# Hybrid attention and recurrence layer: half of the embedding's product moves from attention to the first up products, and six other places are reordered

## The chip, the cores and the metric

The kernel runs on one core of a Trainium2 chip. The metric is the device time of one execution in microseconds (us), the median of some runs. A core has TensorE (PE; its weight loads are PEld), VectorE (DVE), ScalarE (ACT), GpSimd (POOL) and SyncE (SP, which issues the DMAs here). They run side by side and wait for each other by semaphores. Each works through its own instructions in order.

## The reference

One layer on 1024 tokens of width 1024, all in float32:

```
h = rms(x);  c_q, c_kv, k_rope, lru_x, lru_gate = split(h @ w_in)
q, k, v from c_q and c_kv (8 heads, 64 + 32 rotary), RMS norm of q and k per head
attn = softmax(q k^T / sqrt(96), chunk mask) v
lru  = scan(a, b) * gelu(lru_gate)          a, b from two sigmoid gates of conv4(lru_x)
x = x + concat(rms(attn), rms(lru)) @ w_out
x = x + (gelu(g) * v) @ w_down              g, v = conv3(rms(x) @ w_up), 2 x 2816 wide
x = x + sigmoid(rms(x) @ w_gate + b) * (p @ w_ple)       p: 1024 x 256
```

The last product, p @ w_ple, depends on nothing else in the layer. It is called the embedding here.

## The kernel before

Everything is held transposed: 128 features on the partitions, tokens along a row, in two halves of 512 tokens. A float32 operand is split into a high part (`hi`, a ScalarE copy) and a rest (`lo`, a VectorE subtraction), and each product is three matmuls per block of 128 x 128 x 512: hi hi, hi lo, lo hi (`split`, `three`, `chain`, lines 108 to 145). `chain` issues nearly all matmuls, so they carry line 108, and the tile's name tells them apart.

The stages follow each other in `build`. `project` loads x, scales and splits it, adds up its squares (line 255), and multiplies with w_in; `lru` within it runs the recurrent block in four chunks of 128 channels; `qkv` makes queries, keys and values for eight tiles of tokens. `attention` runs eight heads. Per head it transposes q and k (`turn`), makes scores and softmax for eight tiles of queries (`probs`), transposes the probabilities (`turn_probs`) and weighs the values (`weigh`). These are jobs with a time in units, 12 of them for a head (`TURN_AT`, `PROBS_AT`, `BLOCK_AT`, `WEIGH_AT`), and a sort by time gives the order in which they are written. The embedding is among the jobs: `embed(c, h)`, for each of eight blocks c of 128 features and each half h of the tokens, at -1.0 and 3.25 of a head's 12 units. It has 6 matmuls of 512 columns, a copy by ScalarE (line 1197) and a store of 256 KB (line 1198); the results wait in memory until the last stage. `mix` multiplies with w_out: for each half and each of eight blocks, a product over the recurrent part (`lru`), one over the attention part (`at`), each scaled by VectorE and added to x1.

`ffn` makes the up product by seven products instead of eight for each pair of output blocks (Strassen with sums): `order` lists them as (pair u, product 1 to 7). `weights` and `finish_weights` (`W`, `W2`) prepare the w_up operand A, `operand` and `T(n, k)` the x operand B, `sums` adds the products to the outputs U, `run` does a product with its sums. The first 15 products are written out by hand around the operands. `down` runs 22 steps in each half, over eight accumulators that fill all of PSUM, with operands loaded two steps ahead (`load_down`); after a half, `gained` scales and splits x for the last stage, for all eight blocks. `ple` is the gate product, 16 of 24 matmuls. A scale of the RMS norm goes `measure` (TensorE, VectorE, GpSimd: 1/sqrt) and `scale` (VectorE makes a diagonal tile dg, TensorE spreads it, ScalarE copies).

The order written is not the order run in every case. A scheduler in the framework takes the instructions with their priority in the order written, works with estimated durations, gives each engine whatever is ready in that estimate, and assigns buffers. Tiles of one tag share a ring of `bufs` buffers: tag "sq" has 4 (`NTMP`), "wraw" 3, "whi" and "wlo" 2 each, "B" 12. PSUM has eight banks; `banks` names them by stage, and "big" tiles take two.

Of the kernel before, what the change touches and what calls it, by code (L numbers as in the profile page):

```python
# [11 lines left out]
F32 = mybir.dt.float32  # L12
# [34 lines left out]
EMBED_AT = (-1.0, 3.25)  # L47
# [27 lines left out]
class Block:  # L75
# [137 lines left out]
    def project(self):  # L213
# [22 lines left out]
        for k in range(NK):  # L236
# [13 lines left out]
            if k == 0:  # L250
                nc.scalar.activation(ssum, raw, AF.Square)
            else:
                sq = rp.tile([P, S], F32, tag="xsq", name="xsq", bufs=2)
                nc.scalar.activation(sq, raw, AF.Square)
                (nc.gpsimd if k % 2 and k < NK - 1 else nc.vector).tensor_tensor(out=ssum, in0=ssum, in1=sq, op=ALU.add)
# [119 lines left out]
    def lru(self, x, ws, done, then, scale):  # L375
# [43 lines left out]
        for c in range(NL):  # L419
# [131 lines left out]
    def qkv(self, t, c, uq, ukv):  # L551
# [31 lines left out]
        if t == NT - 1:  # L583

            nc.scalar.activation(tmp, tmp, AF.Exp, scale=0.0)
# [20 lines left out]
    def attention(self):  # L606
# [11 lines left out]
        self.pp = [self.wload(self.i["pT"][k]) for k in range(2)]  # L618
        self.e = []
# [6 lines left out]
        mask = self.w.tile([P, S], F32, tag="wraw", name="mask", bufs=3)  # L626
        nc.sync.dma_start(out=mask[QK:QK + NT], in_=self.i["mask"][0])
        for g in range(2):
            nc.scalar.copy(self.qb[g][0][QK:QK + NT], mask[QK:QK + NT, g * HALF:(g + 1) * HALF])
        mask = self.w.tile([P, S], F32, tag="wraw", name="mask", bufs=3)  # L630
        nc.sync.dma_start(out=mask[QK:QK + NT], in_=self.i["mask"][1])
        for g in range(2):
            nc.scalar.copy(self.kb[g][0][QK:QK + NT], mask[QK:QK + NT])
# [4 lines left out]
        jobs = []  # L638
# [19 lines left out]
        self.mix_attn(3, 0)  # L658
# [87 lines left out]
    def mix(self):  # L746
# [13 lines left out]
        for h in range(2):  # L760
# [8 lines left out]
            for c in range(NK + 2):  # L769
                if c < NK:  # L770
# [13 lines left out]
                if c >= 2:  # L784
                    o, x = at[c - 2], self.x1[c - 2][h]
                    V.tensor_tensor(out=o, in0=o, in1=self.r1[:, hs], op=ALU.mult)
                    V.tensor_tensor(out=x, in0=o, in1=x, op=ALU.add)
                    nc.sync.dma_start(out=self.xs[c - 2][:, hs], in_=x)
                    self.square(("x1", h), c - 2, x)
                if h == 1:  # L790
                    if c == 2:
                        self.measure("x1", 0, D)
                        for z, u in ((0, 0), (1, 0), (0, 1)):
                            self.fetch(u, z)
                    if c == 3:

                        self.scale("x1", 0)
                    if 4 <= c < 8:
                        for k in (c - 4, c):
                            self.normed(k, 0)  # L800
                            self.operand(("B21" if k >= NL else "B11", k % NL), self.x1[k][0], self.m[0])
                            self.finish_operand()
# [216 lines left out]
    def ffn(self):  # L1019
# [48 lines left out]
        run(2)  # L1068
        run(3)
        T(1, 0)  # L1070
        T(1, 1)
        W2(7)
        T(1, 2)
        T(1, 3)
# [3 lines left out]
        W2(8)  # L1078
        run(5)
# [72 lines left out]
    def down(self):  # L1152
# [29 lines left out]
    def embed(self, c, h):  # L1182
# [132 lines left out]
```

## Time and profile before

| | |
|---|---|
| median of 3 runs | 1242.09 us (1239.92 to 1243.95) |
| profiled execution: own time, span | 1244.59 us, 1242.8 us |
| VectorE, ScalarE, GpSimd busy | 72%, 52%, 13% of the span |
| mean granted clock of TensorE | 0.984 of full speed |
| DMA | 128.78 MB, 30% of 16 engines' span |

All times of rows are from the start of the span. TensorE's busy time counts matmuls whose ends are modelled and which overlap, so a matmul of 0.39 us may be issued every 0.23. The stages lie about so: front and input products to 164 us, `qkv` to 198, attention to 370, mix to 467, up products to 899, down to 1145, gate to the end.

### The profile page before, as it was taken

Reading aid. Unit: us, or ns where it says so; the run is one execution under the profiler, and the core shown is the slowest. Engines: PE = TensorE matmul, PEld = TensorE weight load, DVE = VectorE, ACT = ScalarE, POOL = GpSimd, SP = SyncE. Lnnn points to the kernel's source line nnn. Section 1 sums busy time; section 2 is a strip of 40 time slices with the busy share of each in tenths; the row PEclk is TensorE's granted clock in tenths of the full one; section 3 lists DMA queues with packets and bytes.
Section 4 is the critical chain, followed back from the end, with each engine's and each line's share of the span. In section 5 each row is a group of like instructions: output and inputs, shape, how many; then the busy total and the mean of one; then the engine's idle time right before and its main releaser. Section 6 shows DMA issues by size and latency. Waiting matters only on the chain.

```text
span 1242.8 us, 15388 instructions
## 1 busy us (share of the span) xinstructions
PE 1201.3 (97%) x5600; PEld 1001.7 (81%) x5600; DVE 896.6 (72%) x1406; ACT 643.6 (52%) x1030; POOL 165.8 (13%) x180
## 2 busy tenths in 40 slices
PE   7999998999999998899999999999999998999998
PEld 5787986888878887788888888888888886888787
DVE  7879798777778699998878878778653346444633
ACT  7388677888874134654544545545432244333211
POOL 3012264444430000000000000000000021001200
PEclk9999998999999998899999999999999998999999
DMA  6213200111168220322222222122485336641221
GB/s 226 68 55 111 103 7 9 48 36 55 43 196 291 86 73 22 107 97 85 85 85 85 69 102 85 68 88 86 132 286 186 106 103 219 202 153 51 69 101 69
DMA packets 49932, 128.78 MB, mean 104 GB/s; under 512 B 5808, under 2 KB 8752, under 8 KB 49856
## 3 DMA queue, kind: packets, MB, share of 16 engines
q1 hardware_dynamic: 49856, 127.80, 30.2%
q8 instruction: 44, 0.72, 0.2%
q14 instruction: 32, 0.26, 0.1%
HBM read 97.36 MB, written 28.31 MB: 101 GB/s over the span
## 4 chain that ended last, share of the span: by engine, by line
PE 66%; DVE 6%; issue 1%; DMA 0%; ACT 0%; POOL 0%; POOLq 0%; DVEq 0%
PE b L108 31%; PE dn L108 16%; PE gt L108 6%; PE lru L108 4%; PE at L108 3%; PE st L108 2%; DVE m L118 1%; DVE B L911 1%; PE big L108 1%; DVE x L1038 1%; DVE x L1177 1%; DVE x L896 0%; PE p L734 0%; PE st L144 0%; DMA om<-oc 0%
## 5 line engine op out<-in xcount | busy, mean ns | idle before, releaser
L108 PE MATMUL b<-B,A 128*128 128x512 f32 x1848 | 424.9, 392 | 3.7 <-DVE U L992 3.4
L108 PEld LDWEIGHTS b<-B,A 128*128 128x128 f32 x1848 | 349.7, 190 | 78.0 <-issue 3.8
L108 PE MATMUL dn<-m,whi 128*128 128x512 f32 x616 | 191.9, 392 | 4.9 <-DVE m L113 4.9
L113 DVE TENSOR_TENSOR wlo<-wraw,whi 128x1024 fp32r<-128x1024 f32 (+2 forms) x59 | 68.1, 1157 | 123.8 <-ACT whi L112 123.8
L108 PEld LDWEIGHTS dn<-m,whi 128*128 128x128 f32 x616 | 116.8, 190 | 29.9 <-DVE m L113 5.4
L112 ACT CAST whi<-wraw 128x1024 fp32r<-128x1024 f32 (+2 forms) x59 | 58.4, 994 | 147.0 <-PE st L108 136.7
L108 PE MATMUL dn<-m,wlo 128*128 128x512 f32 x308 | 120.9, 392 | 0.0
L1004 DVE SCALAR_TENSOR_TENSOR u<-U,par,u 128x1023 f32<-128x1023 f32 x88 | 112.4, 1278 | 2.1 <-ACT u L1009 2.0
L846 POOL TENSOR_TENSOR ssum<-ssum,sq 128x512 f32<-128x512 f32 x14 | 21.4, 1532 | 658.7 <-ACT sq L842 657.9
L944 ACT CAST A<-s 128x512 fp32r<-128x512 f32 x88 | 54.7, 622 | 78.0 <-PE b L108 70.8
L108 PE MATMUL gt<-m,wh 128*128 128x512 f32 (+1 forms) x272 | 80.0, 377 | 0.0
L108 PE MATMUL big<-kT,qT 96*128 96x384 f32 (+11 forms) x288 | 68.7, 365 | 3.5 <-ACT kT L117 3.3
L952 DVE TENSOR_TENSOR A<-s,A 128x512 fp32r<-128x512 f32 x88 | 60.6, 689 | 14.7 <-ACT A L944 14.6
L108 PEld LDWEIGHTS dn<-m,wlo 128*128 128x128 f32 x308 | 58.5, 190 | 12.1
L972 ACT COPY keep<-b 128x512 f32<-128x512 f32 x66 | 38.4, 583 | 52.4 <-PE b L108 52.4
L702 DVE TENSOR_SCALAR_CACHE_REDUCE pr<-big,nrq 128x512 f32<-128x512 f32 (+3 forms) x64 | 51.9, 814 | 11.7 <-PE p L715 4.3
L706 POOL TENSOR_SCALAR pr<-pr,st 128x512 f32<-128x512 f32 (+3 forms) x64 | 48.2, 757 | 78.5 <-DVE st L705 59.9
L944 ACT CAST A<-wraw 128x512 fp32r<-128x512 f32 x54 | 33.4, 622 | 47.8 <-PE b L108 40.5
L108 PEld LDWEIGHTS big<-kT,qT 96*128 96x128 f32 (+1 forms) x288 | 50.3, 198 | 9.1 <-ACT kT L117 3.8
L108 PEld LDWEIGHTS gt<-m,wh 128*128 128x128 f32 x272 | 50.0, 188 | 9.3
L1009 ACT ACTIVATE u<-U,par 128x1024 f32<-128x1024 f32 x44 | 54.7, 1246 | 1.5 <-DVE U L994 0.4
L704 ACT ACTIVATE pr<-pr,st 128x512 f32<-128x512 f32 (+3 forms) x64 | 49.7, 777 | 8.0 <-DVE pr L702 6.8
(327 smaller groups left out, 2289.8 us busy)
## 6 DMA issues: line engine op xcount, KB each, us to landing
wraw<-w_down SPq DMA_DIRECT2D x44, 512.0 KB, 3.4
wraw<-w_up SPq DMA_DIRECT2D x33, 512.0 KB, 3.3
g<-u SPq DMA_DIRECT2D x22, 512.0 KB, 2.6
graw<-g SPq DMA_DIRECT2D x44, 256.0 KB, 4.1
raw<-w_up SPq DMA_DIRECT2D x11, 512.0 KB, 3.4
e<-eo SPq DMA_DIRECT2D x16, 256.0 KB, 2.4
m<-y SPq DMA_DIRECT2D x8, 512.0 KB, 7.2
x<-xT SPq DMA_DIRECT2D x16, 256.0 KB, 7.0
```

Of the source, the lines that this page charges most:

```text
L108: self.nc.tensor.matmul(out, lhsT=w, rhs=x, start=start and n == 0, stop=stop and n == len(terms) - 1, **kw)
L112: self.nc.scalar.copy(hi, src)
L113: (self.nc.gpsimd if pool else self.nc.vector).tensor_tensor(out=lo, in0=src, in1=hi.bitcast(F32), op=ALU.subtract)
L702: V.tensor_scalar(out=pv, in0=sc, scalar1=self.nrq[:, qt, h:h + 1], scalar2=None, op0=ALU.mult, op1=ALU.min, accum_out=st[:, 0:1])
L704: nc.scalar.activation(pv, pv, AF.Exp, bias=st[:, 0:1], scale=-1.0, accum_out=st[:, 1:2])
L706: nc.gpsimd.tensor_scalar(out=pr[:, :kend], in0=pr[:, :kend], scalar1=st[:, 2:3], scalar2=1.0, op0=ALU.mult, op1=ALU.mult)
L846: (nc.gpsimd if pool else nc.vector).tensor_tensor(out=self.ssum[key], in0=self.ssum[key], in1=sq, op=ALU.add)
L944: self.nc.scalar.copy(t[:, :HALF], src)
L952: self.nc.vector.tensor_tensor(out=lo, in0=src, in1=hi.bitcast(F32), op=ALU.subtract)
L972: self.nc.scalar.copy(t, self.bank[u, b])
L1004: tap = lambda z, d: V.scalar_tensor_tensor(out=self.u[u, z][:, d:], in0=self.U[u, z][:, :S - d], scalar=self.col(f"cw{2 - d}", z * NF + u ...
L1009: nc.scalar.activation(t, self.U[u, n], AF.Identity, bias=self.col("cb", n * NF + u), scale=self.col("cw2", n * NF + u))
```

## The change

Half 1 of the embedding leaves attention: `embed(c, 1)` now runs in `ffn`, two blocks at a time, between `run(1)` and `run(5)`, from its own load and split of w_ple. p is loaded by halves (`embedded`). The six other places:

1. The front's sum of squares is added by VectorE alone; GpSimd did three of the seven adds.
2. In the last chunk of `lru`, the second gate's two halves go into one "big" accumulator with one sigmoid.
3. The load of Exp's table (an activation that does nothing else) and two of the four casts of the mask come as jobs behind the first two turns.
4. In `mix`, the `at` product runs one block behind the `lru` product, `mix_attn(3, 0)` comes within the mix, and the scale of x1's first half and its operands come earlier.
5. In `down`, the first half's `gained` is spread over steps 1 to 8 of the second half.
6. In `ple`, the scales come one product later.

```
-EMBED_AT = (-1.0, 3.25)
+EMBED_AT = -1.0
 ...
-                (nc.gpsimd if k % 2 and k < NK - 1 else nc.vector).tensor_tensor(out=ssum, in0=ssum, in1=sq, op=ALU.add)
+                nc.vector.tensor_tensor(out=ssum, in0=ssum, in1=sq, op=ALU.add)
 ...
+                if c == NL - 1 and j:
+                    ps = self.acc("big")
+                    for h in range(2):
+                        hs = slice(h * HALF, (h + 1) * HALF)
+                        self.chain(ps[:, hs], self.three(gw, (xch, xcl), (slice(None), g), (slice(None), hs)))
+                    nc.scalar.activation(o, ps, AF.Sigmoid, bias=self.col(b, c))
-                for h in range(2):
+                for h in range(2 if c < NL - 1 or not j else 0):
 ...
-        if t == NT - 1:
-            nc.scalar.activation(tmp, tmp, AF.Exp, scale=0.0)
 ...
-        self.pp = [self.wload(self.i["pT"][k]) for k in range(2)]
+        self.embedded(0, [self.w.tile([P, S], F32R, tag=t, name="pp", bufs=2) for t in ("whi", "wlo")])
 ...
+        def hide(g):
+            nc.scalar.copy(self.qb[g][0][QK:QK + NT], mask[0][QK:QK + NT, g * HALF:(g + 1) * HALF])
+            nc.scalar.copy(self.kb[g][0][QK:QK + NT], mask[1][QK:QK + NT])
+        def tables():
+            t = self.nv.tile([P, 2, H], F32, tag="htmp", name="tab", bufs=2)
+            nc.scalar.activation(t[:, 0, :], self.mhalf[:, :H], AF.Exp)
+        hide(0)
 ...
-        jobs = []
+        jobs = [(TURN_AT[0] + .1, tables, ()), (TURN_AT[0] + .2, hide, (1,))]
 ...
-            for h in range(2):
-                jobs.append((UNITS * c + EMBED_AT[h], self.embed, (c, h)))
+            jobs.append((UNITS * c + EMBED_AT, self.embed, (c, 0)))
 ...
-        self.mix_attn(3, 0)
 ...
-            for c in range(NK + 2):
+            for c in range(NK + 3):
 ...
-                    at.append(self.acc("at"))
-                    self.chain(at[c], part(c, range(NL)))
-                if c == 1:
+                if h == 0 and c == 1:
+                    self.mix_attn(3, 0)
+                if h == 1 and c == 1:
+                    self.measure("x1", 0, D)
+                if 1 <= c <= NK:
+                    at.append(self.acc("at"))
+                    self.chain(at[c - 1], part(c - 1, range(NL)))
+                if h == 1 and c == 2:
+                    self.scale("x1", 0)
+                    for z, u in ((0, 0), (1, 0), (0, 1)):
+                        self.fetch(u, z)
+                if c == 2:
                     self.measure("at", h, NL * P)
-                if c == 2:
+                if c == 3:
                     self.scale("at", h)
 ...
-                    if c == 2:
-                        self.measure("x1", 0, D)
-                        for z, u in ((0, 0), (1, 0), (0, 1)):
-                            self.fetch(u, z)
-                    if c == 3:
-                        self.scale("x1", 0)
+                    for k in {2: (0,), 3: (1, 2), 4: (3,), 5: (4,), 6: (5,), 7: (6,), 8: (7,)}.get(c, ()):
+                        self.normed(k, 0)
+                        self.operand(("B21" if k >= NL else "B11", k % NL), self.x1[k][0], self.m[0])
+                        self.finish_operand()
                     if 4 <= c < 8:
-                        for k in (c - 4, c):
-                            self.normed(k, 0)
-                            self.operand(("B21" if k >= NL else "B11", k % NL), self.x1[k][0], self.m[0])
-                            self.finish_operand()
                         self.weights(c - 4)
 ...
+        self.embedded(1, [self.up.tile([P, S], F32R, tag="B", name="pp", bufs=3 * NL) for _ in range(2)])
         run(0)
+        run(1)
+        self.measure("x1", 1, D)
         W(4)
+        W2(4)
         W(5)
-        self.measure("x1", 1, D)
-        W2(4)
+        W(6)
+        self.embed(0, 1, "b3")
+        self.embed(1, 1, "b3")
+        self.scale("x1", 1)
         W2(5)
-        run(1)
-        W(6)
         W2(6)
-        self.scale("x1", 1)
         W(7)
+        W2(7)
         run(2)
+        self.embed(2, 1, "b3")
+        self.embed(3, 1, "b3")
         run(3)
-        T(1, 0)
-        T(1, 1)
-        W2(7)
-        T(1, 2)
-        T(1, 3)
+        for k in range(NL):
+            T(1, k)
+        self.embed(4, 1, "b3")
+        self.embed(5, 1, "b3")
         run(4)
         W(8)
         T(2, 0)
         W2(8)
+        self.embed(6, 1, "b3")
+        self.embed(7, 1, "b3")
         run(5)
 ...
+                if h and 1 <= j <= NK:
+                    self.gained(j - 1, 0, "g_ple", "x2", pool=True)
 ...
-            for c in range(NK):
-                self.gained(c, h, "g_ple", "x2", pool=True)
+        for c in range(NK):
+            self.gained(c, 1, "g_ple", "x2", pool=True)
 ...
+    def embedded(self, h, tiles):
+        self.pp = []
+        for k, t in enumerate(tiles):
+            raw = self.n.tile([P, HALF], F32, tag="sq", name="praw", bufs=NTMP)
+            self.nc.sync.dma_start(out=raw, in_=self.i["pT"][k][:, h * HALF:(h + 1) * HALF])
+            self.pp.append((t[:, :HALF], t[:, HALF:]))
+            self.split(raw, *self.pp[k])
+    def embed(self, c, h, tag=None):
 ...
+        if tag:
+            r = self.n.tile([P, HALF], F32, tag="sq", name="eraw", bufs=NTMP)[:, :2 * P]
+        else:
+            r = self.w.tile([P, 2 * P], F32, tag="wraw", name="eraw", bufs=3)
+        nc.sync.dma_start(out=r, in_=self.i["w_ple"][c])
 ...
+        self.split(r, *we, pool=not tag)
+        ps = self.acc(tag) if tag else self.turned()
 ...
+            o = self.n.tile([P, HALF], F32, tag="sq", name="eo", bufs=NTMP)
 ...
-            if n in (1, 4):
+            if n in (2, 5):
                 self.scale("x2", n // 3)
```

## Rows read from the trace of the kernel before

**Rows 1.** The page: TensorE's busy time (share) and instructions; its granted clock in tenths.

```profile
PE 1201.3 (97%) x5600; PEld 1001.7 (81%) x5600; DVE 896.6 (72%) x1406; ACT 643.6 (52%) x1030; POOL 165.8 (13%) x180
...
PEclk9999998999999998899999999999999998999999
```

**Rows 2.** TensorE's waits over the span: us in total, times, longest.

```profile
PE dn L108 <- DVE m L113: 4.9, 1, 4.9
PE big L262 <- DVE xl L118: 4.7, 4, 2.2
PE st L144 <- DVE ssum L846: 3.8, 1, 3.8
PE b L108 <- DVE U L992: 3.4, 1, 3.4
PE big L108 <- ACT kT L117: 3.3, 1, 3.3
PE bc L108 <- ACT b_r L430: 2.8, 1, 2.8
...
PE st L734 <- ACT ph L112: 1.7, 1, 1.7
PE st L164 <- DVE dg L162: 1.3, 1, 1.3
```

**Rows 3.** Stretches: us, busy time of each engine (instructions), PEclk, DMA share, GB/s.

```profile
203.70:210.50 6.80, 6.80 (x26) 5.84 (x25) 3.86 (x14) 3.56 (x10) 2.10 (x4) 0.50 0.10 39
204.00:366.00 162.00, 158.16 (x964) 137.33 (x963) 128.53 (x321) 130.08 (x295) 70.91 (x85) 0.98 0.21 63
371.00:374.40 3.40, 3.40 (x10) 2.61 (x9) 3.40 (x6) 2.40 (x3) 0.26 (x1) 0.50 0.37 93
427.00:445.00 18.00, 18.00 (x88) 15.04 (x88) 12.62 (x26) 3.44 (x6) 2.02 (x2) 1.00 0.12 44
461.80:512.00 50.20, 42.89 (x178) 34.24 (x176) 48.66 (x83) 24.34 (x43) 1.01 (x1) 0.92 0.16 51
...
1033.15:1040.00 6.85, 5.49 (x13) 4.38 (x14) 4.24 (x6) 0.00 (x0) 0.00 (x0) 0.50 0.84 246
1040.00:1140.90 100.90, 100.90 (x446) 83.53 (x446) 39.90 (x41) 34.23 (x41) 0.00 (x0) 1.00 0.46 156
```

**Rows 4.** Chain that ended last, in the up products: start, us, what.

```profile
512.19 386.38 PE b L108 x1692
```

**Rows 5.** Timeline of the front: start, us, engine, line, operation, tiles, shapes.

```profile
11.73 0.75 DVE L113 TENSOR_TENSOR wlo<-wraw,whi 128x256 fp32r<-128x256 f32 x2
...
12.13 2.62 POOL L255 TENSOR_TENSOR yss<-yss,xsq 128x1024 f32<-128x1024 f32 x1 [7.81 <-ACT xsq L254]
12.40 2.37 DVE L366 TENSOR_TENSOR lacc<-lacc,s 128x4 f32<-128x4 f32 x1
...
17.90 1.22 DVE L255 TENSOR_TENSOR yss<-yss,xsq 128x1024 f32<-128x1024 f32 x1
```

**Rows 6.** Timeline of ScalarE ahead of attention's first scores.

```profile
196.21 1.13 ACT L629 CAST qT<-mask 8x512 fp32r<-8x512 f32 x2
...
198.55 1.04 ACT L633 CAST kT<-mask 8x1024 fp32r<-8x1024 f32 x1
199.61 1.28 ACT L585 ACT_TABLE_LOAD   x1
```

**Rows 7.** Timeline of ScalarE at the end of attention.

```profile
367.45 0.72 ACT L117 ACTIVATE m<-at,par 128x512 fp32r<-128x512 f32 x1 [2.44 <-POOL at L742]
```

**Rows 8.** Timeline of SP in the first up products.

```profile
500.67 9.96 SPq L890 DMA_DIRECT2D wraw<-w_up  x3
```

**Rows 9.** Groups between the down product's halves: busy us, mean ns, idle before.

```profile
L846 POOL TENSOR_TENSOR ssum<-ssum,sq 128x512 f32<-128x512 f32 x7 | 10.7, 1536 | 543.1 <-ACT sq L842 542.7
L118 DVE SCALAR_TENSOR_TENSOR m<-x,par,m 128x512 fp32r<-128x512 f32 x8 | 10.6, 1390 | 0.0
```

More of the change, by code (lines that the diff above doesn't have):

```diff
@@ L617, in attention @@
         self.rot, self.obank = ["p0", "p1", "st"], "p2"
-        self.pp = [self.wload(self.i["pT"][k]) for k in range(2)]
-        self.e = []
+        self.embedded(0, [self.w.tile([P, S], F32R, tag=t, name="pp", bufs=2) for t in ("whi", "wlo")])
+        self.e = [self.dr.tile([P, S], F32, name=f"e{c}") for c in range(NK)]
         self.tp = tp
@@ L625, in attention @@
         self.kb = [[tp.tile([QK + NT * (j == 0), S], F32R, name=f"kT{j}{g}") for j in range(2)] for g in range(2)]
[L626 to L633, printed above, removed]
+        mask = [self.w.tile([P, S], F32, tag="wraw", name="mask", bufs=3) for _ in range(2)]
+        for j in range(2):
+            nc.sync.dma_start(out=mask[j][QK:QK + NT], in_=self.i["mask"][j])
+        def hide(g):
[5 more added lines that the diff above has]
+        hide(0)
         self.kT, self.qT = {}, {}
@@ L783, in mix @@
                             self.mix_attn(k, 1)
-                if c >= 2:
-                    o, x = at[c - 2], self.x1[c - 2][h]
+                if c >= 3:
+                    o, x = at[c - 3], self.x1[c - 3][h]
                     V.tensor_tensor(out=o, in0=o, in1=self.r1[:, hs], op=ALU.mult)
                     V.tensor_tensor(out=x, in0=o, in1=x, op=ALU.add)
-                    nc.sync.dma_start(out=self.xs[c - 2][:, hs], in_=x)
-                    self.square(("x1", h), c - 2, x)
+                    nc.sync.dma_start(out=self.xs[c - 3][:, hs], in_=x)
+                    self.square(("x1", h), c - 3, x)
                 if h == 1:
-                    if c == 2:
-                        self.measure("x1", 0, D)
-                        for z, u in ((0, 0), (1, 0), (0, 1)):
-                            self.fetch(u, z)
-                    if c == 3:
-                        self.scale("x1", 0)
+                    for k in {2: (0,), 3: (1, 2), 4: (3,), 5: (4,), 6: (5,), 7: (6,), 8: (7,)}.get(c, ()):
+                        self.normed(k, 0)
+                        self.operand(("B21" if k >= NL else "B11", k % NL), self.x1[k][0], self.m[0])
+                        self.finish_operand()
                     if 4 <= c < 8:
-                        for k in (c - 4, c):
-                            self.normed(k, 0)
-                            self.operand(("B21" if k >= NL else "B11", k % NL), self.x1[k][0], self.m[0])
-                            self.finish_operand()
                         self.weights(c - 4)
@@ L1177, in down @@
                         V.tensor_tensor(out=self.x1[c][h], in0=ps[c], in1=self.x1[c][h], op=ALU.add)
-            for c in range(NK):
-                self.gained(c, h, "g_ple", "x2", pool=True)
+        for c in range(NK):
+            self.gained(c, 1, "g_ple", "x2", pool=True)
         self.c_ff = cg
-    def embed(self, c, h):
-        nc = self.nc
-        if h == 0:
-            r = self.w.tile([P, 2 * P], F32, tag="wraw", name="praw", bufs=3)
-            nc.sync.dma_start(out=r, in_=self.i["w_ple"][c])
-            we = self.ew.tile([P, HALF], F32R, tag="ew", name="ew", bufs=3)
-            self.we = we[:, :2 * P], we[:, 2 * P:]
-            self.split(r, *self.we, pool=True)
-            self.e.append(self.dr.tile([P, S], F32, name=f"e{c}"))
-        hs = slice(h * HALF, (h + 1) * HALF)
-        ps = self.turned()
-        self.chain(ps, [q for k in range(2) for q in self.three(self.we, self.pp[k], (slice(None), slice(k * P, (k + 1) * P)),
-                                                                (slice(None), hs))])
-        o = self.w.tile([P, HALF], F32, tag="wraw", name="eo", bufs=3)
+    def embedded(self, h, tiles):
[5 more added lines that the diff above has]
+            self.split(raw, *self.pp[k])
@@ new lines, in embed @@
+    def embed(self, c, h, tag=None):
+        nc = self.nc
+        if tag:
[3 more added lines that the diff above has]
+        nc.sync.dma_start(out=r, in_=self.i["w_ple"][c])
+        if tag:
+            we = self.up.tile([P, S], F32R, tag="B", name="ew", bufs=3 * NL)
+        else:
+            we = self.ew.tile([P, HALF], F32R, tag="ew", name="ew", bufs=3)
+        we = we[:, :2 * P], we[:, 2 * P:HALF]
+        self.split(r, *we, pool=not tag)
+        ps = self.acc(tag) if tag else self.turned()
+        self.chain(ps, [q for k in range(2) for q in self.three(we, self.pp[k], (slice(None), slice(k * P, (k + 1) * P)),
+                                                                slice(None))])
+        if tag:
+            o = self.n.tile([P, HALF], F32, tag="sq", name="eo", bufs=NTMP)
+        else:
+            o = self.w.tile([P, HALF], F32, tag="wraw", name="eo", bufs=3)
@@ L1197, in embed @@
         nc.scalar.copy(o, ps)
-        nc.sync.dma_start(out=self.e[c][:, hs], in_=o)
+        nc.sync.dma_start(out=self.e[c][:, h * HALF:(h + 1) * HALF], in_=o)
     def ple(self):
```

## The prediction

> **What bounds the kernel now.** I read the page's engine shares first, then TensorE's waits, then the stretches around them. TensorE is busy 97% of the span, and the clock row is full nearly everywhere [rows 1]. So time can come only from fewer matmuls, from TensorE's waits, or from what the clock loses. The waits are few and named [rows 2]: the eight listed make 25.9 us. The reader should then see in the stretches [rows 3] that a wait costs twice: after the wait for kT, and likewise after those for ssum, for U and for the down operand m (the first and the last of these four stretches stand), the granted clock is 0.50 (1.2 instead of 2.4 GHz) for 6.8 us, so 3.4 us more are lost each time. After the one at the end of attention it is 0.50 for 3.4 us, so 1.7 us. In attention itself TensorE is idle 3.8 of 162 us, with VectorE at 79% and ScalarE at 80%. One 512-column matmul at full clock costs 386.38/1692 = 0.228 us [rows 4]. The sum is made against the profiled execution, 1244.59 us (span 1242.8); the median of the runs shown is 1242.09, 2.5 lower.
>
> **Front (ssum adds from GpSimd to VectorE).** Beside a GpSimd add of 2.62 us a VectorE instruction on 128x4 takes 2.37 instead of 0.2, and the next xl waits behind it; VectorE does the same 1024-wide add in 1.22 [rows 5]. The page's timeline holds three such pairs, one for each GpSimd add. VectorE gives back 3 x 2.2 and takes on 3 x 1.2: 3 us less ahead of the last xl. TensorE waits 4.7 us for xl in all [rows 2]. Value -3.0. Ends: -4.7, and +3.4 if the three adds are put ahead of an xl each time.
>
> **Last gate of the recurrent block in one "big" accumulator.** It takes two 512-wide sigmoids off bc and st and adds one 1024-wide. The wait on bc [rows 2] lies at the third block, not at this last one, where TensorE already runs the next product in between. Value 0; ends -1.3 (one table load, 1.28 [rows 6]) and +1.2 (the bank is held by one 1024-wide operation instead of two).
>
> **Start of attention (masks, table).** Just before the first kT ScalarE does two qT mask casts, two kT mask casts, the Exp table load and its use, all ahead of the qT and kT casts [rows 6]; TensorE waits 3.3 us for that kT [rows 2]. Half the mask casts (0.57 + 1.04) and the load (1.28) move behind the first two turns: 2.9 us earlier. They then stand ahead of the first exp, where TensorE has score products to do. With 3.3 - 2.9 = 0.4 us left, the half-clock stretch may go (3.4). I take -3.5; the ends are -6.7, and +2.6 if the table is loaded twice more (second rival). The two splits of p are half as wide (512 instead of 1024) and lie well ahead of this, in VectorE's own time: 0.
>
> **Attention without half of the embedding.** 8 x 6 = 48 matmuls of 0.228 leave: 11.0 us. With them go 8 copies of ScalarE and 8 stores of SP; the 8 loads and splits of w_ple stay. TensorE is the engine without room here [rows 3], so most of it should come off. But these matmuls were put at 3.25 of every 12 units to fill in; ScalarE's 130.1 us less eight copies (some 4.6, by the 0.57 of a 512-wide cast [rows 6]) and VectorE's 128.5 would now stand in 151 us, 83 and 85%, and TensorE will sometimes find no cover. I take two thirds, -7.5; ends 0 and -11.0.
>
> **End of attention.** ScalarE's m<-at idles 2.44 us for GpSimd's at, with two ph casts behind it [rows 7]; TensorE waits 1.7 us for ph and then runs 3.4 us at half clock [rows 2, 3]. That m is mix_attn(3, 0), which now stands behind two products of the mix. Also only one of two whi and wlo buffers is held by p now, so the first w_out tile can be split earlier. But the order on an engine is a planner's, and something else, such as a w_out cast that waits for its DMA, can take that place. Value -1.5; ends 0 and -3.4.
>
> **Mix and first up products.** TensorE gets the 11.0 us. It loses the wait for ssum, 3.8, with its half clock, 3.4, since the second product and two embeddings now cover it, and the wait for U, 3.4 (before, it began at 512.19 - 3.4 = 508.8). So TensorE reaches the product that waits for U at 508.8 + 11.0 - 3.8 - 3.4 = 512.6. VectorE decides the other side: it is busy 48.7 of 50.2 us up to U [rows 3]. It gets eight 256-wide splits of w_ple at 0.375 [rows 5] and two 512-wide of p at 0.69: 4.4 us (GpSimd did the w_ple splits in attention). Back comes idle time: 18 - 12.6 = 5.4 us in 427 to 445 [rows 3], where VectorE waited for the scale of x1's first half, which is now measured one product earlier, with its eight normed and split operands spread over seven steps instead of four. I count 3. U then comes at 512.0 + 1.4 = 513.4, a wait of 0.8 and a start 1.3 later than before. Of the 3.4 us at half clock behind it I take 2.8 as gone: -1.5. Ends: -3.1 (all idle time used: 512.6 against 512.2, no half clock) and +7.5 (the wait for ssum and both half-clock stretches stay: 512.6 + 7.2 against 512.2). Two loads of p, 8 of w_ple and 8 stores go to SP, whose next fetch of w_up is at 500.67 [rows 8], with DMA at 16% [rows 3]; their landing is hidden as long as they are issued early. The stores wait for ScalarE's copy, and the w_up fetches stand behind them: this would show as A waiting.
>
> **Down product.** Between its halves VectorE scales eight x (L118) at 1.39 us each, 10.6 us in one block, beside seven GpSimd adds [rows 9], and the operand m of the next step comes after them: wait 4.9, then 3.4 at half clock [rows 2, 3]. Now one x is scaled in each of the steps 1 to 8 of the second half, which has operands for two steps in store. Value -8.0; ends -8.3 and 0 (worse is the third rival).
>
> **Gate product.** The scale of x2 comes one product later; TensorE's wait of 1.3 for dg [rows 2] lies behind VectorE's scaling block and gets 48 x 0.228/2 = 5.5 us of cover. -1.3; ends 0 and -1.3.
>
> Sum: -3.0 + 0 - 3.5 - 7.5 - 1.5 - 1.5 - 8.0 - 1.3 = -26.3, so 1218.3 for an execution like the profiled one and 1215.8 on the median: 1216.
>
> **Rivals.** First: attention is not set by TensorE alone. Its softmax chain keeps the pace, 1 us comes off instead of 7.5, and VectorE gets no idle time back in the mix: U at 516.4, with its half clock, +4.2 instead of -1.5. Total -26.3 + 6.5 + 5.7 = -14.1: 1228. For it: ScalarE and VectorE at 80%, and an order tuned with these matmuls in it. Against: only 3.8 us of idle TensorE in 162.
>
> Second: the Exp table is loaded before the last square root of the key and query scales. Its activation now reads a constant instead of that root's result, so nothing but a buffer of the ring htmp holds it back. The root's table and Exp's are then loaded once more, 2 x 1.28: +2.6 instead of -3.5 at the start of attention, 1222. The Trainium skill (ScalarE: Activation LUTs, "Table sets: the hidden batching unit") says to finish the calls of one set before the next, since every switch is a load; the row of one load agrees.
>
> Third, on the other side: the second half of the down product becomes VectorE-bound. Two steps take TensorE 48 x 0.228 = 10.9 us. VectorE has three 1024-wide splits at 1.22 and two 512-wide at 0.69, 5.0 us, and now two scalings (0.69) and up to two blocked stretches of a GpSimd add (1.54 [rows 9]): 9.5. It decides from 1.4 us more in two steps; also the squares now share four buffers with the loads of g. If each of eight steps then ends in a wait like that at the end of attention, 1.7 + 1.7, it costs 27.2 and the 8.0 is not gained: -26.3 + 8.0 + 27.2 = +8.9, 1251. Against: VectorE is at 40% in that half [rows 3]. The Trainium skill (SBUF, State Buffer, "Who interferes with whom") speaks for it: VectorE and GpSimd hold a shared port pair for a whole instruction, and the other blocks fully. The 2.37 us in [rows 5] agree. By that rule all seven adds, once beside one block, now stop VectorE in steps that had none.
>
> Fourth: the planner gives the time back elsewhere, and nothing measurable is left: 1242.
>
> **How the numbers follow.** Forecast 0.65, first rival 0.18, second 0.08, third 0.05, fourth 0.04. A measurement of this kernel tells about 0.3%, 4 us, from no change. The forecast, the first two rivals make faster 0.91; the fourth the same, 0.04; the third slower, 0.05. The range runs from 1205 (front, start and attention near their lower ends: 11 below the forecast) to 1233 (the first rival, and nothing from the front and the end of attention: 1228 + 4.5), and leaves the third and fourth out.
>
> **What would show it.** TensorE's wait for the down operand m gone, and no stretch at 0.50 near it; the waits for ssum and kT below 1 us; no GpSimd in the front beyond small ones; attention near 154 us instead of 162; the first up products up to U some 1 us longer. It is wrong if attention keeps its length, if waits for U or A grow beyond 4 us, or if TensorE waits in every step of the second down half.

## The result, and the profile after

The changed kernel takes 1248.88 us (median of 6 runs, 1247.38 to 1251.34), the one before 1243.02 beside it: ratio 1.0053, 95% interval [1.0034, 1.0073]. It is 0.5% slower. The forecast was 1216, with a range that ended at 1233: wrong in sign, and by 33 us.

The profiled execution of the changed kernel has a span of 1246.3 us (before 1242.8), with the same 5600 matmuls. Its page answers to [rows 1] with

```profile
PE 1200.1 (96%) x5600; PEld 998.6 (80%) x5600; DVE 898.9 (72%) x1419; ACT 644.5 (52%) x1038; POOL 158.3 (13%) x177
...
PEclk9998999999999999899999999999999999999999
```

TensorE's busy time is nearly the same (1200.1 us against 1201.3), and the row of its clock has fewer dips: 23.9 us in stretches at 0.50, the tail left out, against 37.6. So idle time must have come in: 46.2 us of the span against 41.5. TensorE's waits, as in [rows 2]:

```profile
PE b L108 <- ACT ew L112: 8.7, 3, 5.6
PE bc L108 <- DVE m L454: 3.9, 1, 3.9
PE t L325 <- DVE cqkv L317: 3.3, 2, 2.6
PE b L108 <- ACT B L913: 2.9, 2, 2.5
...
PE dn L108 <- DVE wlo L113: 2.0, 1, 2.0
```

The waits for m in the down product, ssum, U, kT and xl are gone, as forecast (1.1 us for xh is left in the front). In their place stand four new ones: ew and B in the first up products, m (L454) and cqkv in the recurrent part and behind it. Where that counts is seen by stage. The table has the time between two starts of TensorE's work in the two profiled executions, from the timeline:

| stretch, us | before | after | difference | forecast |
|---|---|---|---|---|
| start to the last kv product | 194.5 | 197.7 | +3.3 | -3.0 |
| from there to the first scores | 7.8 | 8.7 | +1.0 | -3.5 |
| first scores to the last weighting | 168.2 | 158.5 | -9.8 | -7.5 and -1.5 |
| from there to the first up product | 93.8 | 92.5 | -1.3 | |
| first to last up product | 433.9 | 451.9 | +18.0 | -1.5, with the line above |
| from there to the first gate product | 247.4 | 241.9 | -5.4 | -8.0 |
| gate product, first to last | 92.0 | 90.0 | -1.9 | -1.3 |

Attention came out near its forecast, in part by luck, as shown under "Why the prediction was wrong". The up products got 11.0 us of matmuls and lost 7.0 more. The stretches of the changed kernel that answer to [rows 3] (us, busy time of each engine with instructions, granted clock, DMA share, GB/s): kT's, attention, the mix, the first up products, the second down half.

```profile
203.70:207.10 3.40, 3.40 (x12) 2.73 (x13) 2.06 (x4) 3.36 (x5) 0.77 (x2) 0.50 0.00 0
206.50:365.00 158.50, 150.79 (x927) 128.99 (x926) 132.28 (x328) 130.73 (x296) 73.35 (x86) 1.00 0.19 57
428.00:446.00 18.00, 18.00 (x81) 14.86 (x81) 16.78 (x31) 5.39 (x9) 1.38 (x1) 1.00 0.17 59
457.50:505.80 48.30, 34.26 (x138) 24.84 (x136) 39.22 (x70) 20.46 (x40) 1.01 (x1) 0.95 0.35 113
...
1051.00:1150.00 99.00, 99.00 (x438) 81.97 (x438) 39.12 (x42) 33.20 (x40) 0.15 (x1) 1.00 0.45 149
```

VectorE is busy 16.8 of 18 us in the mix now (12.6 before), as hoped. But in the 48.3 us of first up products every engine has room: TensorE is idle for 14.0, VectorE for 9.1, ScalarE for 27.8. Nobody is the bound there; something passes from one to the next too slowly. SyncE's queue shows it, where [rows 8] had only fetches of w_up:

```profile
462.18 4.82 SPq L1217 DMA_DIRECT2D eraw<-w_ple  x2
470.93 0.33 SPq L1232 DMA_DIRECT2D e<-eo  x1
472.61 0.33 SPq L1217 DMA_DIRECT2D eraw<-w_ple  x1
...
500.79 0.33 SPq L1232 DMA_DIRECT2D e<-eo  x1
501.16 0.42 SPq L1217 DMA_DIRECT2D eraw<-w_ple  x1
```

From the third on, each load of a piece of w_ple comes behind the store of an earlier product. ScalarE then waits for the last one with seven casts of B operands queued behind it:

```profile
505.26 0.40 ACT L112 CAST ew<-eraw 128x256 fp32r<-128x256 f32 x1 [3.98 <-DMA eraw<-w_ple]
505.57 3.73 ACT L913 CAST B<-x 128x512 fp32r<-128x512 f32 x7
```

TensorE waits 5.6 us for that cast, and runs at half clock from 504.05 for 6.8.

The earlier loss is in the recurrent part. The first products end 6.9 us earlier than before (113.2 against 120.1), yet the low-rank stage (the product that makes c_q, c_kv and k_rope) begins 0.4 later and takes 44.7 instead of 41.8 us from its first product to its last. VectorE's and GpSimd's rows there (start, us):

```profile
106.36 3.41 DVE L118 SCALAR_TENSOR_TENSOR m<-y,par,b_i 128x1024 fp32r<-128x1024 f32 x1
109.69 2.79 DVE L113 TENSOR_TENSOR w1l<-w1raw,w1h 128x416 fp32r<-128x416 f32 x1
112.40 3.91 DVE L406 SCALAR_TENSOR_TENSOR xc<-u,par,xc 128x1023 f32<-128x1023 f32 x3
...
127.05 2.82 DVE L118 SCALAR_TENSOR_TENSOR m<-y,par,b_i 128x1024 fp32r<-128x1024 f32 x1 [2.38 <-ACT b_i L117]
129.80 0.60 DVE L317 TENSOR_SCALAR cqkv<-a,rx 128x384 f32<-128x384 f32 x1
```

```profile
106.07 2.62 POOL L471 TENSOR_TENSOR yss<-yss,gl 128x1024 f32<-128x1024 f32 x1
108.65 3.38 POOL L447 TENSOR_TENSOR b_i<-b_i,xc 128x1024 f32<-128x1024 f32 x1
123.68 3.26 POOL L447 TENSOR_TENSOR b_i<-b_i,xc 128x1024 f32<-128x1024 f32 x1 [11.65 <-ACT b_i L432]
126.90 1.89 POOL L470 TENSOR_TENSOR gl<-y 128x1024 f32<-128x1024 f32 x1
```

Two rows of VectorE last 3.41 and 2.79 us, each beside a GpSimd row. The conv taps (L406) that TensorE's last gate needs come after them, and the first cqkv comes after a third such row (127.05, beside GpSimd's at 126.90).

### The profile page after: what moved, and what is told of

The parts are those of the page before. It is cut to its first block, busy times and chain, and to the rows that moved or that the text cites. A ratio compares the mean times of both kernels' runs of the same rounds, so it can differ in the third digit from the quotient of the medians.

```text
span 1246.3 us, 15437 instructions
## 1 busy us (share of the span) xinstructions
PE 1200.1 (96%) x5600; PEld 998.6 (80%) x5600; DVE 898.9 (72%) x1419; ACT 644.5 (52%) x1038; POOL 158.3 (13%) x177
## 4 chain that ended last, share of the span: by engine, by line
PE 78%; DVE 11%; ACT 3%; issue 2%; DMA 2%; POOL 2%; SPq 0%; DVEq 0%; POOLq 0%; ACTq 0%
PE b L108 33%; PE dn L108 16%; PE gt L108 7%; PE big L108 4%; PE a L108 3%; PE at L108 2%; PE st L108 2%; PE lru L108 2%; PE big L262 2%; PE p L742 2%; PE p L723 1%; DVE xc L406 1%; DVE m L118 1%; DMA x<-xT 1%; PE p L108 1%
## 5 line engine op out<-in xcount | busy, mean ns | idle before, releaser
L108 PEld LDWEIGHTS dn<-m,wlo 128*128 128x128 f32 x308 | 57.8, 188 | 14.4 <-DVE wlo L113 2.5
```

The lines of the kernel that those rows point to most:

```text
L108: self.nc.tensor.matmul(out, lhsT=w, rhs=x, start=start and n == 0, stop=stop and n == len(terms) - 1, **kw)
```

## The experiments

Each ran 5 rounds beside the kernel before (medians 1242.3 to 1243.3).

**Early loads.** Two transfers read all of w_ple ahead of the stage:

```diff
+        self.eraw = [self.up.tile([P, S], F32, tag="B", name="eraw", bufs=3 * NL) for _ in range(2)]
+        for j in range(2):
+            nc.sync.dma_start(out=self.eraw[j]..., in_=self.i["w_ple"][4 * j:4 * j + 4]...)
-            r = self.n.tile([P, HALF], F32, tag="sq", name="eraw", bufs=NTMP)[:, :2 * P]
+            r = self.eraw[c // 4][:, c % 4 * 2 * P:(c % 4 + 1) * 2 * P]
...
-        nc.sync.dma_start(out=r, in_=self.i["w_ple"][c])
+            nc.sync.dma_start(out=r, in_=self.i["w_ple"][c])
```

> The changed kernel with the eight pieces of w_ple for the first up products read by two transfers into tiles of their own, issued ahead of everything of that stage (they no longer share the ring of four with the embedding's stores). Theory A: each load of w_ple stood on SyncE's queue behind the store of an earlier embedding, so ScalarE's cast came late and TensorE waited 5.6 us at 500 (and ran 3.4 us at half clock after it) and 2.5 us at 488; with the loads ahead both go, and the time falls by 7 to 9 us from 1248.9, to about 1241. Theory B: ScalarE's own queue (casts, copies, B operands) is the bound of that stretch; then the wait moves to the B operands and the time stays at 1246 or above.

1233.19 us, ratio 0.9922 [0.9904, 0.994]: 15.7 faster than the changed kernel, twice what was expected. The up products take 438.0 us instead of 451.9. So the late loads are the cause. That the queue's order made them late was not shown, since this edit also frees the ring.

**Stores from ScalarE's queue.** Queue or ring:

```diff
-        nc.sync.dma_start(out=self.e[c][:, h * HALF:(h + 1) * HALF], in_=o)
+        (nc.scalar if tag else nc.sync).dma_start(out=self.e[c][:, h * HALF:(h + 1) * HALF], in_=o)
```

> The changed kernel with one thing else: the embedding's stores of the first up products are issued from ScalarE's queue, and no longer from SyncE's; the ring of four tiles that w_ple's pieces share with the stores' source stays as it was. Theory A (SyncE's queue is in order, and each load of w_ple stands behind a store that waits for ScalarE's copy): the loads run ahead by themselves, the wait of 5.6 us at 500 and most of those at 484 to 492 go, and the time falls by 8 to 13 us, to 1236 to 1241, a little short of the run with the early loads (1233.2), since ScalarE now issues eight transfers. Theory B (the ring of four: a load waits until an older store has left its tile, whichever queue): the loads still come one by one, and the time stays within 1246 to 1250.

1246.29, ratio 1.0037 [1.0021, 1.0053]. Theory A falls. With no store on SyncE's queue the loads still come one at a time, seven of them over 29.5 us:

```profile
460.84 29.46 SPq L1217 DMA_DIRECT2D eraw<-w_ple  x7
```

In the changed kernel SyncE itself waited for the stores' copies (20.2 us, six times, from 458 to 505). In this run, in the same stretch, it waits in front of the loads, for the other users of the ring: an earlier piece's split, the scale's dg, a store that has landed:

```profile
SPq L1217 <- DVE ew L113: 10.9, 3, 5.0
...
SPq L1217 <- PE st L164: 6.4, 1, 6.4
SPq L1217 <- DMA e<-eo: 3.6, 1, 3.6
```

**Tiles of their own for the stores' source.** The other half of the same question: queue as it was, ring relieved.

```diff
-            o = self.n.tile([P, HALF], F32, tag="sq", name="eo", bufs=NTMP)
+            o = self.eo2[:, c % 2 * HALF:(c % 2 + 1) * HALF]     # eo2, ew2: one "B" tile for two products
```

> The changed kernel with one thing else: in the first up products the stores' source (the copies of the embedding) has tiles of its own, two products to a tile, instead of the ring of four that it shared with w_ple's pieces; the loads of w_ple are still eight, from that ring, on SyncE's queue with the stores. Theory A (the ring: a load of w_ple waits until an older store has left its tile): the loads run ahead, the last of them before 490 instead of 501; the wait of 5.6 us goes and the time falls by 9 to 13 us from 1248.9, to 1236 to 1240. Theory B (the number of small loads, or ScalarE's own queue): the time stays at 1245 or above; only fewer and larger loads ahead of the stage help.

1231.49, ratio 0.9916 [0.9892, 0.9939]: 17.4 faster than the changed kernel. Loads and stores share SyncE's queue, and the loads run ahead all the same:

```profile
459.00 5.65 SPq L1217 DMA_DIRECT2D eraw<-w_ple  x3
...
469.38 4.71 SPq L1217 DMA_DIRECT2D eraw<-w_ple  x4
475.28 12.51 SPq L1235 DMA_DIRECT2D e<-eo  x6
```

So the ring of four "sq" tiles, shared by loads, stores' copies, the copies of the up products and dg, set the pace: a load waited until an older user had left its tile. The up products take 437.4 us, 14.4 less than in the changed kernel. Most of the rest is 2.3 us ahead of attention, where the code is the same: the profiled executions of four kernels with this code there end their kv products between 195.4 and 197.7 us.

**The half back in attention.** The old embed and wload of pT, all else as changed:

```diff
-            jobs.append((UNITS * c + EMBED_AT, self.embed, (c, 0)))
+            for h in range(2):
+                jobs.append((UNITS * c + EMBED_AT[h], self.embed, (c, h)))
```

> The changed kernel with the second half of the embedding's product back in attention as before (whole pT read at once, two products per head); masks, table load, order of the mix, spread of the down stage and the gate as changed. Theory A: in the first up products the embeddings cost their 11 us and 7 us of waiting; in attention they cost about 8 us. So the up stage is 18 us shorter and attention some 8 us longer: 1248.9 - 10 = about 1239. Theory B: the 7 us of waiting come from the new order of scales and weights there and not from the embeddings: up is 11 us shorter only, and the time is 1246 or above.

1236.04, ratio 0.9942 [0.9923, 0.996]. Theory A: the up products take 433.3 us, attention 168.6 (158.5 with the move). The other six edits together are 7 us faster than before; the move as written costs 12.8.

**Gate undone, and gate alone.** The first makes this edit in the changed kernel, the second makes the opposite one in the kernel before:

```diff
-                if c == NL - 1 and j:
-                    ps = self.acc("big")
...
-                for h in range(2 if c < NL - 1 or not j else 0):
+                for h in range(2):
```

> The changed kernel with the last input gate of the recurrent part back in the two small banks (all else as changed). Theory A: the gate moved to a "big" bank is ready some 9 us earlier, so GpSimd multiplies it by xc at 123.7, ahead of y*y and the sum; VectorE's row that scales y (2.82 us beside it) then delays cqkv, and TensorE waits 2.6 us for a transpose and runs 3.4 us at half clock in the low-rank stage. Undone, that stage takes 41.8 us again instead of 44.7, and the time falls by 3 to 5 us from 1248.9, to about 1245. Theory B: the earlier front (the sums of squares all on VectorE) is what shuffles this queue; then the stage still takes 44 us or more and the time stays within 1248 to 1250.

1246.8, ratio 1.0031 [1.0016, 1.0045]. The low-rank stage takes 43.2 us, between the two figures of the theories. The median falls by 2.1 but the intervals overlap: not decided.

> The kernel before with one part of the change alone: the last input gate of the recurrent part in a "big" bank. Theory A (the gate is ready earlier, and VectorE's rows of the last block come before the first row of the low-rank stage, with or without GpSimd beside them): that stage takes 43.5 to 45 us instead of 41.8, and the time is 1244 to 1247 (before: 1242.5). Theory B (it was the earlier front that shuffled the queue, the gate by itself costs nothing, as the prediction had it): 41.8 us again, 1242 to 1243.5.

1246.34, ratio 1.0039 [1.0023, 1.0056]. The gate alone makes the kernel before slower, by 3.3 us of the median. Its executions spread from 1243.8 to 1251.5, and the profiled one is the slowest, so what it shows is the upper end: the low-rank stage takes 45.7 us instead of 41.8, and TensorE waits for cqkv, where before it waited 0.7 in all:

```profile
PE t L325 <- DVE cqkv L317: 4.4, 2, 3.7
```

**Front alone.** In the kernel before:

```diff
-                (nc.gpsimd if k % 2 and k < NK - 1 else nc.vector).tensor_tensor(out=ssum, in0=ssum, in1=sq, op=ALU.add)
+                nc.vector.tensor_tensor(out=ssum, in0=ssum, in1=sq, op=ALU.add)
```

> The kernel before with one part of the change alone: the sums of squares of x all on VectorE. Theory A: the first products end 4 us earlier, but the gain is lost in the last block of the recurrent part, where VectorE beside GpSimd sets the time: 1242.5 to 1243.5, no change that can be told. The prediction's own figure for this part was -3: 1240.

1242.09, ratio 0.9997 [0.9982, 1.0011]. The first products end 9.3 us earlier (110.8 against 120.1), the first query product begins 0.7 earlier. The recurrent part takes nearly all of it.

**Early loads with the old gate, and then without GpSimd.** The second, and the next two, have this edit:

```diff
-            nc.gpsimd.tensor_tensor(out=bx, in0=bx, in1=xc, op=ALU.mult)
+            V.tensor_tensor(out=bx, in0=bx, in1=xc, op=ALU.mult)
...
-                e = V if c == NL - 1 else nc.gpsimd
-                e.tensor_tensor(out=gl, in0=y, in1=y, op=ALU.mult)
-                e.tensor_tensor(out=self.yss, in0=self.yss, in1=gl, op=ALU.add)
+                nc.scalar.activation(gl, y, AF.Square)
+                V.tensor_tensor(out=self.yss, in0=self.yss, in1=gl, op=ALU.add)
```

> The changed kernel with the early loads of w_ple and the last input gate back in the small banks. If the two are independent, the gate's 2 us (1248.9 to 1246.8) come off 1233.2: 1231. If the 4.3 us by which the attention began earlier without the gate edit are kept once the up stage no longer waits, 1229. Rival: the early front's gain is met by the same VectorE queue whatever the gate does: 1233.

1232.77, ratio 0.9921 [0.9906, 0.9936], the same as with the new gate: a miss for both first figures, and the time that the rival named.

> As the run with the early loads and the old gate, and in the recurrent part nothing is left to GpSimd: the squares y*y of blocks 1 to 3 on ScalarE, their sums and the products of the input gate with xc on VectorE (all blocks). Theory A: in the last block VectorE's rows beside GpSimd's took 3.41 and 2.78 us where the same rows take 1.40 and 0.58 us alone; that is why the front's 6.9 us were gone by the low-rank stage. Without GpSimd the wait of 5.5 us for the last block's xch and the half clock after it shrink, and the low-rank stage begins 3 to 5 us earlier: about 1227. Theory B: VectorE has no room for the additional 10 operations of 1.2 us each; the waits move to the earlier blocks and the time is the same or up to 5 us more than without this edit.

1222.29, ratio 0.9836 [0.9817, 0.9856]: 10.5 faster by this edit. Eight operations leave GpSimd (the ten of the expectation was a miscount), VectorE takes six of them and gives one to ScalarE. Its rows, with GpSimd silent, are far shorter than those above:

```profile
98.30 1.28 DVE L118 SCALAR_TENSOR_TENSOR m<-y,par,b_i 128x1024 fp32r<-128x1024 f32 x1 [0.72 <-ACT b_i L117]
99.50 1.22 DVE L463 TENSOR_TENSOR yss<-yss,gl 128x1024 f32<-128x1024 f32 x1
100.64 1.22 DVE L403 TENSOR_TENSOR u<-big,rb 128x1024 f32<-128x1024 f32 x1
101.77 1.58 DVE L113 TENSOR_TENSOR w1l<-w1raw,w1h 128x416 fp32r<-128x416 f32 x3
103.27 1.22 DVE L440 TENSOR_TENSOR b_i<-b_i,xc 128x1024 f32<-128x1024 f32 x1
104.41 3.91 DVE L406 SCALAR_TENSOR_TENSOR xc<-u,par,xc 128x1023 f32<-128x1023 f32 x3
```

The low-rank stage begins at 111.9 instead of 119.8. From the last block's u (L403) to its conv taps (L406) it is 3.8 us here and 8.5 in the run before it (103.06 to 111.59), where the rows of 3.41 and 2.78 us beside GpSimd stand in between: 4.8 of the 7.9 us. How the rest divides is not shown. GpSimd is also slower at the same work (b_i<-b_i,xc takes it 3.38 us, VectorE 1.22), and that alone would shorten the chain.

> The kernel before with the recurrent part's work taken from GpSimd (squares on ScalarE, sums and b_i*xc on VectorE) and nothing else. Theory A: VectorE beside GpSimd is late in the last block already there; the low-rank stage begins earlier, but by less than in the changed kernel, since the first products still end 4 us later: 1243 - 5 = 1238 (range 1235 to 1240). Theory B: without the earlier front there is nothing to gain: 1242 to 1243.5.

1239.38, ratio 0.9978 [0.9962, 0.9994]: 3.0 faster, the first query product 1.9 earlier. So the edit is worth 3.0 here and 10.5 in the changed kernel. The earlier front is the likely reason (the first products end at 116.5 here, at 108.1 there), but no run has only these two edits.

> As the run of 1222.3 (early loads of w_ple, recurrent part without GpSimd), but with the changed kernel's last input gate in a "big" bank. Theory A: the gate edit cost 2 to 4 us only because it brought GpSimd's product b_i*xc forward, beside VectorE's rows; without GpSimd there it costs nothing: 1221.5 to 1223. Theory B: the gate in a "big" bank costs by itself (one sigmoid over 1024 columns later, the bank held longer): the low-rank stage takes 43.5 us or more instead of 41.7, and the time is 1224 to 1227.

1222.85, ratio 0.9842 [0.9816, 0.9868]. The time is theory A's. In the profile the stage takes 42.6 us against 41.7, between the theories, and TensorE waits 2.2 for cqkv. What the gate costs beside other edits, 0 to 2 us, stays open.

**Down part alone.** In the kernel before:

```diff
+                if h and 1 <= j <= NK:
+                    self.gained(j - 1, 0, "g_ple", "x2", pool=True)
...
-            for c in range(NK):
-                self.gained(c, h, "g_ple", "x2", pool=True)
+        for c in range(NK):
+            self.gained(c, 1, "g_ple", "x2", pool=True)
```

> The kernel before with one part of the change alone: the first half's gate operands spread over units 1 to 8 of the second down product. Theory A: the wait of 4.9 us and the half clock after it go, a wait of 2 us for a split weight comes in their place: 1243.0 - 5.5 = 1237.5. The prediction's own figure for this part was -8: 1235. Rival: VectorE, held by GpSimd's additions of squares, bounds the second half: 1243 or slower.

1239.09, ratio 0.996 [0.9945, 0.9974]: -4.2. The wait of 4.9 becomes one of 2.0, with 3.4 us at half clock at 1036.96.

**All repairs, with the move and without it.** The edits of the stores' tiles, the gate and GpSimd together; then the same with the half back in attention instead of the stores' tiles.

> The changed kernel with the three repairs: the stores' source of the embedding in tiles of its own, the last gate as before, the recurrent part without GpSimd. The run with early loads and the same two others took 1222.3; tiles for the stores' source alone were 1.7 us better than early loads (1231.5 against 1233.2). If they add: 1219 to 1221. If not: 1222 to 1224.

1220.79, ratio 0.983 [0.9811, 0.985]: the fastest run, 22 us under the kernel before and 28 under the changed one. The longest three of TensorE's waits follow. Its clock is at 0.50 only for 3.4 us, from 455.3, and in the tail.

```profile
PE st L233 <- ACT ones_r L207: 2.4, 1, 2.4
PE b L108 <- ACT ew L112: 2.4, 1, 2.4
PE p L734 <- ACT ph L112: 2.2, 4, 0.6
```

> The same with the half of the embedding's product back in attention (gate as before, recurrent part without GpSimd, all else as changed). Theory A: with the ring repaired the move is worth what the prediction gave it, attention -7.5 and up +3.8, so 3 to 4 us: this kernel 3 to 4 us slower than the one before it in this list, about 1224. Theory B: the up stage has idle time of its own that the move only exposes, and the move is worth nothing even when repaired: both within 1.5 us.

1224.87, ratio 0.9858 [0.9839, 0.9876]. The move is worth 4.1 us once its loads are not held up (the executions of the two kernels overlap a little: 1219.2 to 1223.7 and 1222.5 to 1226.3). Attention is 9.7 shorter, the up products 4.5 longer. Theory A. The pair without the other repairs agrees: 1236.0 with the half in attention, 1231.5 with the move and the stores' tiles.

**Two waits more.** In the run of 1222.3, embeddings one product later and pT's first half read early; the split of pT's second half also moves, behind W2(6):

```diff
-        self.embed(0, 1, "b3")
-        self.embed(1, 1, "b3")
         self.scale("x1", 1)
...
         run(2)
+        self.embed(0, 1, "b3")
+        self.embed(1, 1, "b3")
         run(3)
...
-            raw = self.n.tile([P, HALF], F32, tag="sq", name="praw", bufs=NTMP)
+            raws = [self.w.tile([P, HALF], F32, tag="wraw", name="praw", bufs=3) if PRAW and not h else
+                    self.n.tile([P, HALF], F32, tag="sq", name="praw", bufs=NTMP) for _ in range(2)]
```

> The run of 1222.3 and two things more: in the first up products the embeddings stand later by one product of the feed-forward (TensorE waited 4.6 us for the first of them, with operands of the feed-forward ready), and the first half of pT is read into the ring of large weight tiles, free since the recurrent part (TensorE waited 1.3 us for its cast at the start of attention, and the mask tables and first turns stood around it). If both waits go: 1222.3 - 4.8 - 1.5 = 1216, and half of a stretch at half clock. If the wait moves to the weights of the feed-forward behind it: 1220 to 1222.

1222.14, ratio 0.9831 [0.9805, 0.9856]. A miss for 1216: the scores begin 1.9 us earlier, but the wait for ew becomes one, not for the weights that the other branch named, but for the scale of x1,

```profile
PE st L165 <- DVE dg L163: 5.1, 1, 5.1
```

with 6.8 us at half clock after it.

## Why the prediction was wrong

**Mix and first up products: the failed step.** It read: "their landing is hidden as long as they are issued early". Nothing made them early. The loads, the stores' source, the copies of the up products and dg take turns in four tiles; I had seen that buffers were shared in the third rival, for the down product, and did not count them here. The term was -1.5 with ends -3.1 and +7.5; it measured +16.7 (mix and up products). With the ring relieved it measures +1.8 (92.04 + 437.43 - 93.82 - 433.88), inside the ends. That VectorE decides this stretch was wrong as well: it was idle for 9.1 us. With the ring relieved it is busy 43.9 of 47.7 us (454.3 to 502.0 in eo_own), yet the longest wait there, 2.4, is still for ScalarE's ew. The ring relieved and nothing else gives 1231.5: inside the range, but 15.5 above the forecast, for the reasons that follow. The sign named for trouble with the queue was A waiting; it did not come, since TensorE waited for the embedding's own operand first. Of the signs of being wrong (attention's length, U or A, every step of down) none came either.

**Front.** The step itself was right: no GpSimd add is left, VectorE's 1024-wide add takes 1.22 as in [rows 5], and the last xl product starts 4.0 us earlier. Passing -3.0 on to the end was not: front_only shows none of it. The next place that VectorE holds up, the last block of the recurrent part, was not looked at. There GpSimd stretches VectorE's rows as [rows 5] shows. The Trainium skill (SBUF, State Buffer, "Who interferes with whom") has VectorE and GpSimd lock a shared port pair against each other; 3.41 us beside GpSimd and 1.28 without it agree.

**Last gate.** Costed 0, with +1.2 at worst. Alone it costs 3.3. The gate is ready earlier, and with it VectorE's scaling of y (m<-y at 127.05, after 2.4 us for ScalarE) stands ahead of the first cqkv, and with the gate alone as well (132.02, then 133.78). In the kernel before, cqkv came first:

```profile
128.02 0.62 DVE L317 TENSOR_SCALAR cqkv<-a,rx 128x384 f32<-128x384 f32 x1 [1.16 <-PE a L108]
128.55 1.36 DVE L118 SCALAR_TENSOR_TENSOR m<-y,par,b_i 128x1024 fp32r<-128x1024 f32 x1
```

**Start of attention.** The -3.5 did not come (+1.0). The kT wait went, and half its half clock, but what the prediction put at 0 as lying "well ahead of this" came in between: the loads of pT wait for the same ring, and their casts stand among the turns that they should precede,

```profile
201.40 0.60 ACT L112 CAST pp<-praw 128x512 fp32r<-128x512 f32 x1
201.91 0.58 ACT L112 CAST qT<-p 96x512 fp32r<-96x512 f32 x1
203.02 0.62 ACT L112 CAST pp<-praw 128x512 fp32r<-128x512 f32 x1 [0.53 <-DMA praw<-pT]
...
204.24 1.28 ACT L641 ACT_TABLE_LOAD   x1
```

With pT read whole, in half_back, the stretch is 6.1 us instead of 8.7, so the halves cost 2.6. The rest of the -3.5 is not simply there either: half_back has no half clock left at this place, where the kernel before lost 3.4 us inside attention, and its attention is still 0.4 longer. So what was won ahead of the first scores was lost again behind them; at which row is open. The table was loaded once, after the last root (201.28), so the second rival is out.

**Attention and its end.** -9.0 forecast, -9.8 measured, but the near match is in part luck. 3.1 of the 9.8 us are the half clock behind kT: it lay within this stretch (203.7 to 210.5), and now it ends 0.6 us after the first scores (207.1). The prediction booked it under the start. Beside half_back, which has the other edits, the move itself takes 10.2 off attention, and 9.7 in the repaired pair: nearly all of the 11.0, not two thirds. TensorE's idle time there rose from 3.8 to 7.7 us, at 83% VectorE (costed: 85%), and the m<-at that idled 2.44 us [rows 7] now starts without idle time. The first rival, a softmax chain that keeps the pace, is out.

**Down and gate product.** -8.0 forecast, -5.4 measured, alone -4.2: a wait of 2.0 for a split weight stands where 4.9 stood. The scalings are 739 ns each in place of 1390 [rows 9], and the adds take the same:

```profile
L856 POOL TENSOR_TENSOR ssum<-ssum,sq 128x512 f32<-128x512 f32 x7 | 10.8, 1542 | 110.6 <-ACT sq L852 110.5
L118 DVE SCALAR_TENSOR_TENSOR m<-x,par,m 128x512 fp32r<-128x512 f32 x9 | 6.4, 739 | 0.0
```

The third rival, VectorE as the bound there, is out. The gate product gained 1.9 for 1.3.

So the kernel was slower for a reason that no rival named, and 0.05 for slower was too little: each rival priced an engine or an order, none a buffer. One sum of the prediction does not come out: the lower ends of front, start and attention lie 8.4 below the forecast, not 11, so the range began too low; the result lies at its other side.

## What to carry to other kernels

When work moves, write down for each new load which tile it lands in and who gives that tile back; a ring shared by loads and by the source of stores turns independent steps into a chain, whatever queue issues them. Time won ahead of a stage counts only up to the next engine that bounds it, so follow it to that engine's rows before adding it to a sum. An operand made ready earlier can push other work back on an in-order engine.

## What the hardware showed that I had not expected

Taking eight 1024-wide operations off GpSimd and giving VectorE six of them made the changed kernel with early loads and the old gate 10.5 us faster. VectorE's rows beside them had been two to five times as long (3.41 against 1.28 us, 2.79 against 0.53), and where these rows stood, 4.8 of the 7.9 us were won by which the low-rank stage began earlier. The rest is not divided. And the length of a wait does not tell what the clock does behind it: the wait of 2.0 us for wlo in the down product has no stretch at 0.50 near it in the changed kernel, and one of 3.4 us with the down part alone. Code is not the difference: the run with early loads has the changed kernel's down product, the same wait of 2.0, and 3.4 us at 0.50 from 1033.5.
